# Feature-major x for the first projection of a two-layer hybrid trunk, loaded in blocks beside the first weights on a second DMA queue

## The chip, the core and the metric

The kernel runs on one core of a Trainium2 chip. The metric is the device time of one execution in microseconds (us); each version is run several times and the median is compared. Engines are named as in the profile: PE (TensorE matmul), PEld (TensorE weight load), DVE (VectorE), ACT (ScalarE), POOL (GpSimd), SP (SyncE, which here only issues DMAs). A `q` behind an engine's name (SPq, ACTq) means its instruction queue issuing DMAs.

## The reference

A residual stream `h` of 256 tokens by 1024 features (float32) goes through two layers: a dilated-attention mixer, a SwiGLU FFN, a forgetting-attention mixer, a second FFN, and a final RMSNorm. The change touches the first projection alone:

```python
def rmsnorm(x, g):
    y = xf * lax.rsqrt(jnp.mean(xf * xf, axis=-1, keepdims=True) + RMS_EPS) * g
    return y

def dilated_mixer(h, w_in, w_out):
    proj = (h @ w_in).reshape(B, S, N_GROUPS, 3, N_HEADS, HEAD_DIM)   # 1024 x 9216 weights
    ...

for i in range(DEPTH):
    ...
        h = h + dilated_mixer(rmsnorm(h, a_norm[j]), a_w_in[j], a_w_out[j])
    ...
return rmsnorm(h, final_norm)
```

## The kernel before, in words

**Precision.** Every float32 product is made of three matmuls in the fast fp32r type (`mm3`): each operand is split into a rounded high part and a remainder, and high x high, high x low and low x high are summed. So each block of weights, once landed in a `raw` tile, is "cut": ACT copies it to `wh` (L71) and DVE subtracts to get `wl` (L72).

**Weights.** `piece` loads one 1 MB block of weights into two `raw` tiles of 512 KB and cuts them. `raw` has 5 buffers, `wh` and `wl` 4 each. `weights` hands out a block and issues the load of the ones up to two ahead. The first projection consists of 36 units of 256 output columns (`a_units`): the first two, called unit 0 and unit 1 here, are the values of the second and third dilation group; from unit 2 on come queries and keys. For one unit, `proj_tok` runs 2 token tiles x 8 depth blocks x 3 matmuls = 48 matmuls of 256 columns.

**The beginning.** The norm's gain `g_a` is multiplied into x while it is transposed; the per-token factor 1/rms (`r_a`) is applied later, where the projections leave PSUM (L229) and in the rotary tables (`rb`, L459: a matmul that broadcasts `r_a` over partitions with the identity `ident`). The x rows (permuted, `x_perm`, tiles `xp0` and `xp1`, two DMAs of 256 KB each) are transposed on PE in 16 blocks of 128x128 (L310). ACT scales them out of PSUM into the high part of `xt` (L313) and DVE makes the low part (L315). Unit 0's weights are loaded in four parts of 256 KB and cut through the list `cuts`, two after each half tile. After the first token tile's transposes, the first halves of units 0 and 1 (`lead`) run; then come the second tile's transposes and the second halves. The sums of squares for `r_a` (`sq`, ACT, L147, then POOL, L138 and L141) are placed with `tc.issue_after(last.ins)`, where `last` is the last ACT scaling of x: on the engine of that instruction, ACT, nothing of the block may stand ahead of it. A few matmuls on a zeroed tile (`warm_up`, L278) run before data is there.

**What sets the order.** The program is written in one order, and a scheduler then orders the instructions of each engine by priority and by its own estimate of when inputs are ready; `first()` and `tc.high_priority` raise priorities. The resulting order is fixed: each engine runs its list strictly in that order, and an instruction that waits holds up all behind it on that engine. A DMA is issued from the list of its engine (SP before the change for all loads), so a load too can stand behind a waiting instruction.

Of the kernel before, what the change touches and what calls it, by code (L numbers as in the profile page):

```python
# [31 lines left out]
def trunk(ctx: ExitStack, tc: tile.TileContext, T, out):  # L32
# [39 lines left out]
            nc.vector.tensor_tensor(view(lo), src, view(hi).bitcast(F32), op=ALU.subtract)  # L72


    def piece(key, parts=2, todo=None):
        if key[0][:2] == "dn" and key[1] == LATE:
            wh, wl = (y.rearrange("p k c -> p (k c)") for y in fm_tile("ot", KT, 1))
        else:
            wh, wl = (wp.tile([P, 2048], F32R, tag=y, name=y, bufs=4) for y in ("wh", "wl"))
        n = 1024  # L80
        for c in range(2):
            raw = wp.tile([P, n], F32, tag="raw", name="raw", bufs=5)
            m = 2 * n // parts
            for i in range(parts // 2):
                v, u = slice(i * m, (i + 1) * m), slice(c * n + i * m, c * n + (i + 1) * m)
                nc.sync.dma_start(raw[:, v], T[key[0]][key[1]][:, u])
                cut = lambda raw=raw, v=v, u=u: split((wh, wl), lambda y: y[:, u], raw[:, v], False)
                if todo is None:
                    cut()
                else:  # L90
                    todo.append(cut)
        return wh, wl
# [124 lines left out]
    def values_a(v, g, o):  # L217

        if g == 0:
            v[0] = v_tile(o, [rt[:, t:t + 1] for t in range(2)])  # L220
            return
        for a in range(2):
            if 1 + a not in v:
                v[1 + a] = ap.tile([P, 512], F32, tag="v", name="v", bufs=6)
            rows = slice(a * 64, a * 64 + 64)
            with first():
                for t in range(2):
                    s = slice(t * S, (t + 1) * S)
                    nc.scalar.activation(v[1 + a][(g - 1) * 64:g * 64, s], o[rows, s], AF.Copy, scale=r_a[t][rows])  # L229

    def exps(s, nm, den, j):
        nc.scalar.activation(s, s, AF.Exp, bias=nm[:, j:j + 1], accum_out=den[:, j:j + 1])  # L232
# [43 lines left out]
    def warm_up(n):  # L276
        for i in range(n):
            nc.tensor.matmul(o[:, :S], warm[:, :P], warm[:, P:P + S], start=True, stop=True)  # L278

    warm_up(3)  # L280
    with tc.high_priority(offset=1000):
        nc.scalar.activation(warm[:, P + S:P + S + 1], mhalf, AF.Square)

    ident = const("ident", [P, P])
    xperm = [hrow(f"xp{t}") for t in range(2)]

    def load_x(t):
        for i in range(2):
            nc.sync.dma_start(xperm[t][:, i * 512:(i + 1) * 512],
                              T["x_perm"][t * P:(t + 1) * P, i * 512:(i + 1) * 512])  # L290

    load_x(0)
    g_a = const("g_a", [P, KT])
    cuts = []
    ready[order[0]] = piece(order[0], 4, cuts)
    state["next"] = 1
    load_x(1)
    xt = xt_tile()

    r_a = []  # L300

    def scaled_t(t):
        for half in range(2):
            tr = psum("tr")
            hi, lo = xt
            ks = range(half * 4, half * 4 + 4)
            c = slice(t * P, (t + 1) * P)
            src = {k: tr[:, k % 4 * P:(k % 4 + 1) * P] for k in ks}
            for k in ks:
                tp = nc.tensor.transpose(src[k], xperm[t][:, k * P:(k + 1) * P], ident)  # L310
            with first():
                for k in ks:
                    last = nc.scalar.activation(hi[:, k, c], src[k], AF.Copy, scale=g_a[:, k:k + 1])  # L313
                for k in ks:
                    nc.vector.scalar_tensor_tensor(lo[:, k, c], src[k], g_a[:, k:k + 1], hi[:, k, c].bitcast(F32),  # L315
                                                   op0=ALU.mult, op1=ALU.subtract)
                for _ in range(min(2, len(cuts))):
                    cuts.pop(0)()
        if t == 0:
            with tc.issue_after(tp.ins):  # L320
                warm_up(4)
        return last

    for t in range(2):
        last = scaled_t(t)
        if t == 0:
            lead = []
            for i in range(2):
                wt = weights("a_in", a_units[i][1] * 3 + 2)
                lead.append((wt, psum("mm")))  # L330
                proj_tok(xt, wt, lead[i][1][:, :S], 0)
    with tc.issue_after(last.ins):
        for t in range(2):
            r_a.append(rstd([sq(xperm[t])]))
# [104 lines left out]
    for i, (hq, g, w) in enumerate(a_units):  # L439
        if i % 9 == 0:  # L440
            quad = {"hq": hq, "fm": {}, "pt": {}, "v": {}, "nm": stat_tile("nm", 24), "den": stat_tile("den", 24)}
        wt, o = lead[i] if i < 2 else (weights("a_in", hq * 9 + g * 3 + w), psum("mm"))
        if i == 1:
            rcos = const("rcos", [P, S])
            rsin = const("rsin", [P, S])
# [7 lines left out]
        if w < 2:  # L453
            for c in range(2):
                proj_feat(xt, wt, o[:, c * S:(c + 1) * S], c)
            if i == 2:
                rb = psum("tr")
                for t in range(2):
                    nc.tensor.matmul(rb[:, t * P:(t + 1) * P], r_a[t].to_broadcast([P, P]), ident,  # L459
                                     start=True, stop=True)  # L460
                for c in (rcos, rsin):
                    nc.vector.tensor_tensor(c, c, rb[:, :S], op=ALU.mult)
                rt = ap.tile([P, 2], F32, tag="rt", name="rt", bufs=1)
                tmp = ap.tile([P, D], F32, tag="xn", name="rd", bufs=2)[:, :S].rearrange("p (b c) -> p b c", b=2)
                e = early(rb[:, :S], None)
                nc.vector.tensor_tensor(tmp, e, ident[:, None, :].to_broadcast([P, 2, P]), op=ALU.mult)
                nc.vector.tensor_reduce(rt, tmp, axis=AX.X, op=ALU.add)
            q = rotated(o, f"fm{w}", nc.vector if g == 0 else nc.gpsimd)
            if g == 0:
                y = ap.tile([P, 2, 2, S], F32R, tag="h", name="qkr", bufs=4)  # L470
                f, q = q, (y[:, 0], y[:, 1])
                split(q, lambda y: y, f)
            quad["fm"][g, w] = q
            if w == 1:
                later(i + 1, scores_a, quad, g)
                if g == 2:
# [390 lines left out]
```

## Time and profile before

| what | value |
|---|---|
| device time, median of 3 runs | 806.12 us (805.39 to 806.36) |
| profiled execution, its own time | 805.15 us |
| span of its trace | 803.4 us |
| PE busy | 787.4 us (98%) |
| DVE busy | 555.4 us (69%) |
| ACT busy | 421.2 us (52%) |
| data moved by DMA | 135.00 MB, mean 168 GB/s |

The span runs from the first to the last recorded instruction; 1.75 us of the execution lie around it. PE busy is an upper reading, since matmuls are pipelined and overlap in the record. The first 22.3 us of the span hold the beginning described above: loads, transposes, and units 0 and 1.

### The profile page before, as it was taken

To read this page: it belongs to the slowest core of one execution; us is meant where nothing else is said; L and a number is where in the kernel's file an instruction comes from. 1 tells how busy PE (TensorE), PEld (TensorE's weight loads), DVE (VectorE), ACT (ScalarE), POOL (GpSimd) and SP (SyncE) were. 2 spreads that over 40 slices of the span, in tenths; PEclk is the share of its full clock that TensorE was granted. 3 is DMA by queue.
4 is the path that set the end of the run, shared out by engine and by line. 5 is a ranking of instruction groups with operands and counts; after the bars stand their busy time and mean duration, and the time that the engine had idled before them with its cause. 6 is when DMAs were issued, how large, how long until landed. Compare 5 with 4: busy or idle time off the path is not lost.

```text
span 803.4 us, 13954 instructions
## 1 busy us (share of the span) xinstructions
PE 787.4 (98%) x5564; PEld 702.4 (87%) x5564; DVE 555.4 (69%) x829; ACT 421.2 (52%) x819; POOL 59.9 (7%) x76
## 2 busy tenths in 40 slices
PE   8999999999999999999999999999999999999996
PEld 7989899899999789888888879988879888888885
DVE  6798997986986685555657555677766756556643
ACT  7756347447445365455556545364535655546532
POOL 0010111011010110000000001211111000000001
PEclk9999999999999999999999999999999999999999
DMA  8856253734634346655556434543316665655601
GB/s 293 271 158 217 79 184 109 251 106 141 211 130 159 105 162 211 208 180 189 179 205 230 165 133 146 184 171 130 95 40 236 212 207 171 198 179 205 218 1 52
DMA packets 38833, 135.00 MB, mean 168 GB/s; under 512 B 4592, under 2 KB 5360, under 8 KB 38768
## 3 DMA queue, kind: packets, MB, share of 16 engines
q1 hardware_dynamic: 38624, 133.85, 49.9%
q8 instruction: 43, 0.70, 0.3%
q10 hardware_dynamic: 144, 0.26, 0.1%
q14 instruction: 22, 0.18, 0.1%
HBM read 133.05 MB, written 1.05 MB: 167 GB/s over the span
## 4 chain that ended last, share of the span: by engine, by line
PE 82%; DVE 10%; ACT 3%; issue 3%; DMA 1%; SPq 0%; POOL 0%; POOLq 0%; DVEq 0%
PE ps_mm L167 10%; PE ps_mm L169 10%; PE ps_mm L168 10%; PE ps_tr L198 9%; PE ps_mm L198 9%; PE ps_tr L199 4%; PE ps_mm L199 4%; PE ps_sc L167 4%; PE ps_sc L168 4%; PE ps_sc L169 4%; DVE wl L72 4%; PE ps_o L167 3%; PE ps_o L168 3%; PE ps_o L169 3%; ACT wh L71 2%
## 5 line engine op out<-in xcount | busy, mean ns | idle before, releaser
L72 DVE TENSOR_TENSOR wl<-raw,wh 128x1024 fp32r<-128x1024 f32 (+1 forms) x242 | 299.7, 1256 | 133.9 <-ACT wh L71 133.7
L71 ACT ACTIVATE wh<-raw 128x1024 fp32r<-128x1024 f32 (+1 forms) x242 | 248.3, 1048 | 165.2 <-issue 51.6
L167 PE MATMUL ps_mm<-xt,wh 128*128 128x256 f32 x512 | 147.4, 288 | 0.0
L168 PE MATMUL ps_mm<-xt,wh 128*128 128x256 f32 x512 | 145.4, 284 | 0.0
L169 PE MATMUL ps_mm<-xt,wl 128*128 128x256 f32 x512 | 145.4, 284 | 0.0
L198 PE MATMUL ps_tr<-xt,wh 128*128 128x512 f32 x304 | 109.6, 400 | 0.0
L198 PE MATMUL ps_mm<-xt,wh 128*128 128x512 f32 x304 | 108.1, 396 | 0.0
L167 PEld LDWEIGHTS ps_mm<-xt,wh 128*128 128x128 f32 x512 | 97.9, 191 | 3.1 <-issue 2.3
L168 PEld LDWEIGHTS ps_mm<-xt,wh 128*128 128x128 f32 x512 | 98.0, 191 | 1.5 <-issue 1.5
L169 PEld LDWEIGHTS ps_mm<-xt,wl 128*128 128x128 f32 x512 | 97.9, 191 | 1.0 <-issue 1.0
L167 PE MATMUL ps_mm<-wh,xt 128*128 128x256 f32 x304 | 86.6, 285 | 0.8 <-ACT wh L71 0.8
L168 PE MATMUL ps_mm<-wl,xt 128*128 128x256 f32 x304 | 86.0, 284 | 0.3 <-DVE wl L72 0.3
L169 PE MATMUL ps_mm<-wh,xt 128*128 128x256 f32 x304 | 85.8, 283 | 0.0
L199 PE MATMUL ps_tr<-xt,wl 128*128 128x256 f32 x304 | 85.1, 280 | 0.0
L199 PE MATMUL ps_mm<-xt,wl 128*128 128x256 f32 x304 | 84.9, 279 | 0.0
L198 PEld LDWEIGHTS ps_tr<-xt,wh 128*128 128x128 f32 x304 | 57.1, 188 | 15.1 <-DVE low L557 1.5
L198 PEld LDWEIGHTS ps_mm<-xt,wh 128*128 128x128 f32 x304 | 57.1, 188 | 13.2
L232 ACT ACTIVATE p<-p,nm 128x64 f32<-128x64 f32 (+2 forms) x128 | 51.4, 407 | 29.3 <-DVE nm L241 17.9
L167 PEld LDWEIGHTS ps_mm<-wh,xt 128*128 128x128 f32 x304 | 58.5, 192 | 1.7 <-ACT wh L71 1.4
L168 PEld LDWEIGHTS ps_mm<-wl,xt 128*128 128x128 f32 x304 | 58.4, 192 | 0.7 <-DVE wl L72 0.5
L169 PEld LDWEIGHTS ps_mm<-wh,xt 128*128 128x128 f32 x304 | 58.4, 192 | 0.0
L199 PEld LDWEIGHTS ps_mm<-xt,wl 128*128 128x128 f32 x304 | 57.2, 188 | 0.5
(213 smaller groups left out, 1271.5 us busy)
## 6 DMA issues: line engine op xcount, KB each, us to landing
raw<-in_gu SPq DMA_DIRECT2D x88, 512.0 KB, 4.3
raw<-in_a_in SPq DMA_DIRECT2D x70, 512.0 KB, 4.6
raw<-in_dn SPq DMA_DIRECT2D x44, 512.0 KB, 4.0
raw<-in_b_in SPq DMA_DIRECT2D x24, 512.0 KB, 4.6
raw<-in_a_out SPq DMA_DIRECT2D x8, 512.0 KB, 3.6
raw<-in_b_out SPq DMA_DIRECT2D x8, 512.0 KB, 3.5
grow<-in_norms SPq DMA_DIRECT2D x4, 512.0 KB, 5.6
xp<-in_x_perm SPq DMA_DIRECT2D x4, 256.0 KB, 4.6
```

Of the source, the lines that this page charges most:

```text
L71: nc.scalar.activation(view(hi), src, AF.Copy)
L72: nc.vector.tensor_tensor(view(lo), src, view(hi).bitcast(F32), op=ALU.subtract)
L167: nc.tensor.matmul(o, sh, mh, start=start, stop=False)
L168: nc.tensor.matmul(o, sh, ml, start=False, stop=False)
L169: return nc.tensor.matmul(o, sl, mh, start=False, stop=stop)
L198: nc.tensor.matmul(o.rearrange("p (x s) -> p x s", x=2), wh, xt.full[:, k], start=k == 0, stop=False)
L199: nc.tensor.matmul(o[:, :S], wl, xt[0][:, k], start=False, stop=k == KT - 1)
L232: nc.scalar.activation(s, s, AF.Exp, bias=nm[:, j:j + 1], accum_out=den[:, j:j + 1])
```

## The change

The host hands over x a second time, laid out feature-major (`x_fm`: 128 partitions of features, 8 depth blocks of 256 tokens). It is loaded on SP in four parts of 256 KB (two depth blocks each) into tiles `xf0` and `xf1`, behind `g_a`. Unit 0's weights, in four parts of 256 KB, are issued from ACT instead of SP (`piece` gets a parameter `eng`). The 16 transposes are gone: for each depth block, ACT scales x from `xf` into the high part of `xt`, DVE makes the low part, and every second block one part of unit 0's weights is cut. Unit 0 is written depth block by depth block for both token tiles, into two PSUM tiles (`lead`, tag `sc`); unit 1 is now an ordinary unit. `ident` and the token-major x (`xp0`, `xp1`, now one 512 KB DMA each) are still loaded, behind `x_fm`, since the sums of squares and the broadcast use them. The squares are still inside `tc.issue_after(last.ins)`, but `last` is now the last matmul of unit 0, a PE instruction. There are four warm-up matmuls instead of three and four.

```diff
-    def piece(key, parts=2, todo=None):
+    def piece(key, parts=2, todo=None, eng=nc.sync):
...
-                nc.sync.dma_start(raw[:, v], T[key[0]][key[1]][:, u])
+                eng.dma_start(raw[:, v], T[key[0]][key[1]][:, u])
...
-                    nc.scalar.activation(v[1 + a][(g - 1) * 64:g * 64, s], o[rows, s], AF.Copy, scale=r_a[t][rows])
+                    src = o[t][rows, :S] if isinstance(o, list) else o[rows, s]
+                    nc.scalar.activation(v[1 + a][(g - 1) * 64:g * 64, s], src, AF.Copy, scale=r_a[t][rows])
...
-    warm_up(3)
+    warm_up(4)
     with tc.high_priority(offset=1000):
         nc.scalar.activation(warm[:, P + S:P + S + 1], mhalf, AF.Square)
 
+    xf = [hrow(f"xf{i}") for i in range(2)]
+    g_a = const("g_a", [P, KT])
+    for i in range(4):
+        c = slice(i % 2 * 512, i % 2 * 512 + 512)
+        nc.sync.dma_start(xf[i // 2][:, c], T["x_fm"][:, i * 512:(i + 1) * 512])
+    cuts = []
+    w0 = piece(order[0], 4, cuts, nc.scalar)
+    ready[order[1]] = piece(order[1])
+    state["next"] = 2
+    xt = xt_tile()
+
+    r_a = []
+    lead = [psum("sc") for _ in range(2)]
+    hi, lo = xt
+    for k in range(KT):
+        src = xf[k // 4][:, k % 4 * S:(k % 4 + 1) * S]
+        with first():
+            nc.scalar.activation(hi[:, k], src, AF.Copy, scale=g_a[:, k:k + 1])
+            nc.vector.scalar_tensor_tensor(lo[:, k], src, g_a[:, k:k + 1], hi[:, k].bitcast(F32),
+                                           op0=ALU.mult, op1=ALU.subtract)
+            if k % 2 == 0:
+                cuts.pop(0)()
+        for t in range(2):
+            last = mm3(lead[t][:, :S], both(xt, ALL, k, slice(t * P, (t + 1) * P)),
+                       both(w0, ALL, slice(k * 256, (k + 1) * 256)), k == 0, k == KT - 1)
     ident = const("ident", [P, P])
     xperm = [hrow(f"xp{t}") for t in range(2)]
-
-    def load_x(t):
-        for i in range(2):
-            nc.sync.dma_start(xperm[t][:, i * 512:(i + 1) * 512],
-                              T["x_perm"][t * P:(t + 1) * P, i * 512:(i + 1) * 512])
-
-    load_x(0)
-    g_a = const("g_a", [P, KT])
-    cuts = []
-    ready[order[0]] = piece(order[0], 4, cuts)
-    state["next"] = 1
-    load_x(1)
-    xt = xt_tile()
-
-    r_a = []
-
-    def scaled_t(t):
...
-        if t == 0:
-            with tc.issue_after(tp.ins):
-                warm_up(4)
-        return last
-
     for t in range(2):
-        last = scaled_t(t)
-        if t == 0:
-            lead = []
-            for i in range(2):
-                wt = weights("a_in", a_units[i][1] * 3 + 2)
-                lead.append((wt, psum("mm")))
-                proj_tok(xt, wt, lead[i][1][:, :S], 0)
+        nc.sync.dma_start(xperm[t], T["x_perm"][t * P:(t + 1) * P, :])
     with tc.issue_after(last.ins):
         for t in range(2):
             r_a.append(rstd([sq(xperm[t])]))
...
-        wt, o = lead[i] if i < 2 else (weights("a_in", hq * 9 + g * 3 + w), psum("mm"))
+        if i == 0:
+            o = lead
+        else:
+            wt, o = weights("a_in", hq * 9 + g * 3 + w), psum("mm")
...
-            for t in range(i < 2, 2):
+            for t in range(2 if i else 0):
                 proj_tok(xt, wt, o[:, t * S:(t + 1) * S], t, g == 0)
...
+    t["x_fm"] = x[perm].T.reshape(KT, P, S).transpose(1, 0, 2).reshape(P, KT * S)
```

How the scheduler orders the engines' lists changes with it, at three places. From unit 2 on, the lists of the two kernels are almost the same. A number behind a name is the tile's own: `raw_88`, `raw_91` (before) and `raw_89`, `raw_92` (now) hold unit 0's weights, cut to `wh_86` and `wh_87`; `raw_137`, `raw_141` and `raw_97`, `raw_101` unit 1's, cut to `wh_135` and `wh_95`.

ACT before, from its first x scaling on:

```order
L313 ACTIVATE xt_96<-ps_tr_97,g_a_84 128x128 x4
L313 ACTIVATE xt_96<-ps_tr_114,g_a_84 128x128 x4
L71 ACTIVATE wh_86<-raw_88 128x512 x2
L71 ACTIVATE wh_86<-raw_91 128x512 x2
L313 ACTIVATE xt_96<-ps_tr_215,g_a_84 128x128 x4
L71 ACTIVATE wh_135<-raw_137 128x1024
L313 ACTIVATE xt_96<-ps_tr_228,g_a_84 128x128 x4
L71 ACTIVATE wh_135<-raw_141 128x1024
L71 ACTIVATE wh_145<-raw_147 128x1024
L147 ACTIVATE junk_241,ssq_242<-xp0_80 128x1024
```

ACT now, from its start on:

```order
L86 DMA raw_89<-in_a_in 128x512
L283 ACT_TABLE_LOAD
L283 ACTIVATE warm_71<-mhalf_67 128x1
L86 DMA raw_89<-in_a_in 128x512
L303 ACTIVATE xt_105<-xf0_79,g_a_81 128x256 x4
L303 ACTIVATE xt_105<-xf1_80,g_a_81 128x256 x4
L86 DMA raw_92<-in_a_in 128x512 x2
L147 ACTIVATE junk_186,ssq_187<-xp0_182 128x1024
L147 ACTIVATE junk_192,ssq_193<-xp1_183 128x1024
L71 ACTIVATE wh_95<-raw_97 128x1024
L71 ACTIVATE wh_87<-raw_89 128x512 x2
L71 ACTIVATE wh_87<-raw_92 128x512 x2
```

Unit 0's cuts stood directly behind the first tile's scaling; now all of x's scaling, the issue of unit 0's last two parts, both squares of the token-major x and the cut of unit 1's first half stand ahead of them. The squares stood behind three cuts of 1024 columns.

SP now, the loads in the order of their issue:

```order
L60 DMA g_a_81<-in_g_a 128x8
L290 DMA xf0_79<-in_x_fm 128x512 x2
L290 DMA xf1_80<-in_x_fm 128x512 x2
L60 DMA ident_180<-in_ident 128x128
L314 DMA xp0_182<-in_x_perm 128x1024
L314 DMA xp1_183<-in_x_perm 128x1024
L86 DMA raw_97<-in_a_in 128x1024
L86 DMA raw_101<-in_a_in 128x1024
```

The 1 MB of token-major x, which stood in two halves around unit 0's weights, now stands between the feature-major x and unit 1's weights.

PE now, its first rows (`ps_sc_106` and `ps_sc_107` are unit 0's two token tiles, `ps_mm_228` is unit 1, `rs_189` and `rs_195` are `r_a`):

```order
L279 MATMUL ps_o_73<-warm_71 128x256 x4
L445 MATMUL ps_tr_348<-ident_180,rs_189 128x128
L445 MATMUL ps_tr_348<-ident_180,rs_195 128x128
L167 MATMUL ps_mm_228<-wh_95,xt_105 128x256
L167 MATMUL ps_sc_106<-wh_87,xt_105 128x256
L167 MATMUL ps_sc_107<-wh_87,xt_105 128x256
L168 MATMUL ps_mm_228<-wl_96,xt_105 128x256
L169 MATMUL ps_mm_228<-wh_95,xt_105 128x256
L167 MATMUL ps_mm_228<-wh_95,xt_105 128x256
L168 MATMUL ps_mm_228<-wl_96,xt_105 128x256
L169 MATMUL ps_mm_228<-wh_95,xt_105 128x256
L168 MATMUL ps_sc_106<-wl_88,xt_105 128x256
```

Before, PE had 3 warm-ups, 8 transposes and 4 warm-ups ahead of unit 0's first matmul, and the broadcast of `r_a` stood inside unit 2. Now the broadcast of both `r_a` stands ahead of every projection matmul, and eight matmuls of units 0 and 1 stand ahead of the one that needs unit 0's first low part (`wl_88`); 88 of the 96 matmuls of the two units come from there on. On DVE the low part of unit 1's first half (`wl_96`) stands directly ahead of unit 0's four low parts (`wl_88`).

More of the change, by code (lines that the diff above doesn't have):

```diff
@@ L284, in trunk @@
     ident = const("ident", [P, P])
     xperm = [hrow(f"xp{t}") for t in range(2)]
-    def load_x(t):
-        for i in range(2):
-            nc.sync.dma_start(xperm[t][:, i * 512:(i + 1) * 512],
-                              T["x_perm"][t * P:(t + 1) * P, i * 512:(i + 1) * 512])
-    load_x(0)
-    g_a = const("g_a", [P, KT])
-    cuts = []
-    ready[order[0]] = piece(order[0], 4, cuts)
-    state["next"] = 1
-    load_x(1)
-    xt = xt_tile()
-    r_a = []
-    def scaled_t(t):
[L303 to L318, printed above, removed]
-        if t == 0:
-            with tc.issue_after(tp.ins):
-                warm_up(4)
-        return last
```

## The prediction, written before the changed kernel was run

> **What bounds the kernel now.** I read the page first (busy time and the chain of waits), then the table of windows, then the timeline of the first 23 us engine by engine.
>
> ```profile
> PE 787.4 (98%) x5564; PEld 702.4 (87%) x5564; DVE 555.4 (69%) x829; ACT 421.2 (52%) x819; POOL 59.9 (7%) x76
> PE 82%; DVE 10%; ACT 3%; issue 3%; DMA 1%; SPq 0%; POOL 0%; POOLq 0%; DVEq 0%
> ```
>
> ```profile
> 0.00:22.30 22.30, 19.05 (x126) 17.02 (x126) 12.52 (x27) 15.82 (x35) 2.26 (x10) 1.00 0.84 289
> 22.30:40.00 17.70, 17.70 (x149) 17.70 (x149) 15.26 (x23) 12.73 (x16) 0.00 (x0) 1.00 0.80 273
> 40.00:60.00 20.00, 19.85 (x170) 17.49 (x169) 18.60 (x27) 10.83 (x24) 3.81 (x3) 1.00 0.52 159
> 80.00:100.00 20.00, 18.95 (x161) 17.00 (x159) 19.39 (x32) 7.25 (x14) 3.33 (x3) 1.00 0.24 80
> ```
>
> The second number in a window's row is its length, the third PE's busy time. PE carries 82% of the chain, and from 22.3 us it has nothing idle until 40 and 0.15 us until 60. So whatever moves the start of unit 2 moves the end by about as much. The beginning is worth looking at, and there it is the start of unit 2 that I have to time.
>
> ```profile
> 1.30 2.93 PE L278 MATMUL ps_o<-warm 128*128 128x256 f32 x6 [1.30 <-DVE warm L273]
> 5.34 1.89 PE L278 MATMUL ps_o<-warm 128*128 128x256 f32 x8
> 8.03 0.38 PE L167 MATMUL ps_mm<-wh,xt 128*128 128x256 f32 x1 [0.79 <-ACT wh L71]
> 8.75 0.39 PE L168 MATMUL ps_mm<-wl,xt 128*128 128x256 f32 x1 [0.34 <-DVE wl L72]
> 10.55 0.44 PE L310 MATMUL ps_tr<-ident,xp 128*128 128x128 f32 x2 [0.82 <-DMA xp<-in_x_perm]
> 22.14 0.28 PE L168 MATMUL ps_mm<-wl,xt 128*128 128x256 f32 x1
> 22.26 0.28 PE L169 MATMUL ps_mm<-wh,xt 128*128 128x256 f32 x1
> 22.38 0.32 PE L167 MATMUL ps_mm<-xt,wh 128*128 128x256 f32 x1
> ```
>
> A timeline row is start, duration, engine, line. Unit 0 begins at 8.03 and unit 2 at 22.38. Matmuls of 256 columns start 0.12 us apart (22.14, 22.26, 22.38), so the 96 matmuls of units 0 and 1 need 11.5 us of the 14.35; the second tile's transposes and waits take the rest. At most 2.8 us could be had between these two marks, and a little by an earlier start.
>
> **The change part by part.** The diff reads as if the blocks of x and of weights arrived in pairs and PE began with the first pair. The order of the engines' lists says otherwise: unit 0's first cut on ACT stands behind both squares of the token-major x and behind the cut of unit 1's first half, and PE's first matmul behind the broadcast of `r_a`. Strictly ordered lists make PE's start wait for the seventh load on SP, `raw_97`. So I time that load.
>
> Loads. What did the beginning move, and when did it land?
>
> ```profile
> 4.46 0.91 SPq L289 DMA_DIRECT2D xp<-in_x_perm  x2
> xp<-in_x_perm SPq DMA_DIRECT2D x1, 256.0 KB, 6.2
> raw<-in_a_in SPq DMA_DIRECT2D x1, 512.0 KB, 7.7
> 4.00:5.00 1.00, 1.00 (x6) 0.80 (x6) 0.00 (x0) 0.00 (x0) 0.00 (x0) 1.00 0.86 245
> 5.00:6.00 1.00, 1.00 (x8) 0.92 (x8) 0.00 (x0) 0.79 (x4) 0.00 (x0) 1.00 0.49 74
> 6.00:7.00 1.00, 1.00 (x6) 0.76 (x4) 0.61 (x3) 1.00 (x6) 0.00 (x0) 1.00 0.74 168
> 10.00:11.00 1.00, 0.45 (x4) 0.46 (x5) 0.96 (x2) 0.51 (x1) 0.00 (x0) 1.00 1.10 406
> 13.00:14.00 1.00, 1.00 (x10) 0.94 (x9) 0.87 (x4) 1.00 (x3) 0.00 (x0) 1.00 1.04 426
> ```
>
> The last number of a load's row is the time from issue to landing in us, that of a window GB/s. The last part of x (second of the two from 4.46, so issued near 4.9) landed 6.2 us later, at 11.1, when 64 + 4 + 1024 + 1024 = 2116 KB had been asked for up to it. Now SP asks for the same 2116 KB up to the end of `xp1`, but unit 0's weights come on top from ACT: 512 KB early, 512 KB after x's scaling. Those 512 to 1024 KB (0.52 to 1.05 MB) take 1.3 to 2.6 us at 0.41 MB/us: `xp1` lands at 12.4 to 13.7, I take 13.0. `raw_97`, 0.52 MB more, lands 1.25 us later, at 14.2. From below: the dip to 74 and 168 GB/s between 5 and 7 us costs about 1.4 us against its neighbours (2 us at 121 instead of some 400 is 0.56 MB, at 400); if it doesn't come back, 12.8, and with the last 512 KB behind it 12.2. From above: `raw_97` can't be issued before `xf1`'s first part has freed its DMA semaphore, near 7.5, and the slowest 512 KB load here took 7.7: 15.2. That ACT takes four issues off SP is worth nothing, because SP's list is not what is late.
>
> The Trainium skill says the same of the second queue (DMA: Bandwidth & Descriptors, "Issuing engines are not separate DMA queues"): loads from different engines share the same 16 DMA engines, and only sequencer time is saved; by the opposite view the token-major x would not delay unit 0's weights at all, yet the sum here would stay, since it hangs on `raw_97`, which is on SP's own queue.
>
> ACT, DVE, POOL. Their prices stand in these rows:
>
> ```profile
> 7.34 0.63 ACT L71 ACTIVATE wh<-raw 128x512 fp32r<-128x512 f32 x1
> 12.97 1.08 ACT L71 ACTIVATE wh<-raw 128x1024 fp32r<-128x1024 f32 x1
> 16.81 1.11 ACT L147 ACTIVATE junk<-xp 128x1024 f32<-128x1024 f32 x1
> 17.85 1.10 ACT L71 ACTIVATE wh<-raw 128x1024 fp32r<-128x1024 f32 x1
> 8.01 0.69 DVE L72 TENSOR_TENSOR wl<-raw,wh 128x512 fp32r<-128x512 f32 x1
> 14.17 1.22 DVE L72 TENSOR_TENSOR wl<-raw,wh 128x1024 fp32r<-128x1024 f32 x1
> 20.08 0.19 POOL L138 TENSOR_SCALAR rs<-ssq 128x1 f32<-128x1 f32 x1 [0.70 <-ACT junk L147]
> 20.35 0.55 POOL L141 TENSOR_TENSOR rs<-rs,mhalf 128x1 f32<-128x1 f32 x1
> ```
>
> The second square, from 13.0, takes 1.04 us to the next ACT instruction (16.81 to 17.85): 14.1. The cut of unit 1's first half begins with its landing, 14.2, and ends at 15.3 (1.08); `r_a` comes meanwhile (0.19 + 0.55 plus gaps, 15.0). Then unit 0's first high part: 15.9. DVE: `wl_96` 15.3 to 16.5 (1.22), then unit 0's first `wl_88` until 17.2 (0.69, before the overlap of neighbours; I take 17.1). That is the moment that decides. ACT delivers the further parts of unit 0 every 0.55 to 0.63 us and DVE every 0.6 to 0.69, while PE uses one for 12 matmuls, 1.44 us, so nothing more is late; the last weights of unit 1 land near 15.5 and are cut by 20.2, and PE wants them after 23.
>
> PE. 88 matmuls from 17.1 at 0.12 us are 10.6 us: unit 2 at 27.7 instead of 22.38, +5.3 us. The removed transposes (the second tile's eight, some 1 us of the old stretch) are in that difference already, and so are the warm-ups, which end before data is there.
>
> The clock. The six warm-up rows at the start took 2.93 us (0.49 each), the eight later ones 1.89 us (0.24 each): an array that comes from idling runs at half pace for its first 3 to 4 us. Now the warm-ups end near 5 and PE idles for 10 us. No row shows what that does, as PE never idles that long later; the nearest is the start. Like there, matmuls would cost 0.24 instead of 0.12 from 15.3 to near 19, of which 2 to 2.5 us lie behind 17.1: a loss of about half, 1.2 us. Bounds: 0 (the profile's granted clock stands at 1.00 in every window) and 2.0 (4 us, all after 17.1). I take 1.2, since the warm-up rows are the same array after the same kind of pause. Sum: +6.5 us.
>
> The Trainium skill has a rule for that (TensorE: Matmul & The Clock Gate, Part 1: The HAM clock gate): after an idle window of about 3.4 us the clock falls to half and needs as long of activity to return. By it the loss would be some 1.7 us, an estimate, and the sum +7.0; the start's rows agree with it, and no row here shows the fall after a pause.
>
> What could come back later? Loads go on while PE waits, so units 2 to 4 would be cut earlier, relative to PE, than before. But PE was not waiting for cuts from 22.3 to 60 anyway; the 1.05 us missing between 80 and 100 could shrink at most. I count nothing.
>
> Result: 805.15 + 6.5 = 811.65 us for the profiled execution's kind; that one lies 0.97 below the median of 806.12, so 812.6 for the median.
>
> **The rivals.** *The pairs arrive as the diff reads, and it is faster.* If the first part of x and of weights sufficed, PE could begin near 6 (both land near 4, then 0.63 and 0.69 for the cut), unit 0 would end near 12, and unit 1, free to follow, near 18: -4.5 us, 801.6. The mechanism must bring `raw_97` and `xp1` early, since ACT's list puts them ahead: to break even, the 88 matmuls must start at 22.38 - 10.6 = 11.8, so `raw_97` must land at 8.9. By then 3.2 MB would have to be in, of which the best rate here, 426 GB/s, brings 3.0 MB from 2 us on. Chance 3%, with 2% for a tie.
>
> *Two queues fill better and the clock holds.* The dip at 5 to 7 us stood behind the small `g_a` load and may be due to it or to first touches; now `g_a` goes first. With `raw_97` at 12.2 everything up to PE moves 2 us, and without the slow clock the sum is +3.3 us, 809.4; either one alone gives 810.6 to 811.4. For it: windows of over 400 GB/s later. Against: every load has as many bytes ahead as before or more. Chance 28%.
>
> *Later still.* `raw_97` at 15.2 and 2.0 us of slow clock: +8.3, 814.4; a new wait in the first units on top (the PSUM tiles `sc` of unit 0 are emptied on ACT behind the weights' cuts) could bring 816. Chance 12%.
>
> **How the numbers follow.** Main case 55% (811.5 to 813.7), early 28%, late 12%, faster 3%, tie 2%. A difference of 0.2%, 1.6 us here, is what a measurement of this kernel can tell from none; every slower case lies beyond it. So slower 0.95, same 0.02, faster 0.03. The range reaches from just below the early case to the late one with its extra wait: 809.0 to 816.0. It leaves out the two small cases on the other side and the tails of early and late.
>
> **What would show it.** In the changed profile ACT's first cut must be that of unit 1 (1024 columns), behind the two squares, near 14; PE idle from about 5 to about 15; the first unit 0 matmul with `wl` near 17; unit 2 near 28 to 29. The clock shows in the starts of the first matmuls: 0.24 apart if I am right, 0.12 if not. The loads' step is wrong if `raw_97` lands before 12 or after 15.5, and the whole is wrong if unit 0's matmuls start before 11.8. The span from unit 2 on should be as long as before (803.4 - 22.4 = 781.0 us); if it is shorter by more than 1 us, the delay was partly won back and my "nothing" was wrong.

## The result, and the profile after

| | before | changed |
|---|---|---|
| device time, median of 6 runs each | 805.75 us (804.86 to 806.36) | 809.57 us (808.62 to 810.58) |
| profiled execution | 805.15 us | 810.58 us |
| span of its trace | 803.4 us | 808.8 us |

The ratio is 1.0044, with a 95% interval of 1.0031 to 1.0058. The changed kernel is slower by 3.8 us; the prediction had +6.5 us and a range from 809.0 to 816.0. First the page of the changed kernel, the busy time:

```profile
PE 786.5 (97%) x5542; PEld 701.9 (87%) x5542; DVE 554.5 (69%) x821; ACT 420.3 (52%) x811; POOL 59.0 (7%) x76
```

PE has 0.9 us less to do (787.4 before) in a span that is 5.4 us longer: the work did go away, and PE's idle time grew by 6.3 us, from 16.0 (803.4 - 787.4) to 22.3. The table of windows shows where (start and end, length, then the busy time of PE, PEld, DVE, ACT and POOL, the granted clock, the DMA share and GB/s):

```profile
10.00:19.00 9.00, 5.32 (x20) 4.53 (x21) 4.67 (x8) 7.04 (x12) 1.49 (x4) 0.50 0.86 322
28.80:40.00 11.20, 11.20 (x96) 11.20 (x95) 9.77 (x12) 7.00 (x10) 0.00 (x0) 1.00 0.88 312
40.00:60.00 20.00, 20.00 (x149) 18.33 (x149) 17.50 (x27) 11.13 (x24) 2.60 (x2) 1.00 0.55 181
```

From 28.8 to 60 us PE has nothing idle, as before from 22.3. All that is lost is lost ahead of unit 2, and from 10 to 19 the granted clock stands at 0.50, where every window of the kernel before that the prediction shows has 1.00. The timeline of PE in that stretch (start, duration, engine, line; in brackets the idle time and what ended it):

```profile
13.22 0.79 PE L445 MATMUL ps_tr<-ident,rs 128*128 128x128 f32 x2 [8.13 <-POOL rs L141]
...
17.49 0.41 PE L168 MATMUL ps_sc<-wl,xt 128*128 128x256 f32 x1
17.70 0.41 PE L169 MATMUL ps_sc<-wh,xt 128*128 128x256 f32 x1
...
19.55 0.28 PE L167 MATMUL ps_sc<-wh,xt 128*128 128x256 f32 x1
19.67 0.28 PE L168 MATMUL ps_sc<-wl,xt 128*128 128x256 f32 x1
```

PE idles 8.13 us behind its warm-ups, since the broadcast of `r_a` stands first in its list. The first unit 0 matmul with a low part starts at 17.49 (foretold: 17.1). Matmuls start 0.21 us apart until 19.41, then 0.12. Unit 2's first matmul is at 28.89. What ACT did meanwhile:

```profile
11.10 1.06 ACT L147 ACTIVATE junk<-xp 128x1024 f32<-128x1024 f32 x1 [0.95 <-DMA xp<-in_x_perm]
...
13.89 2.62 ACT L71 ACTIVATE wh<-raw 128x1024 fp32r<-128x1024 f32 x4 [0.38 <-DMA raw<-in_a_in]
```

Its first cut, at 13.89, is that of unit 1's first half (1024 columns lead the group), behind both squares, and it waited for that load: `raw_97` landed at 13.9. Unit 0's first weights had been there since 4.2, as the first row of the chain of waits shows (start, length, what):

```profile
0.72 3.50 DMA raw<-in_a_in
4.23 8.10 DMA xp<-in_x_perm
12.36 1.16 ACT junk L147 x2
...
14.48 0.80 PE ps_tr L445 x2
```

By the chain, the second half of the token-major x (landed at 12.3), its square and the broadcast of `r_a` release PE; the cut of `raw_97` (13.89 + 1.08 = 14.97) is level with them. Two paths end at 15.0, which matters for the first experiment that takes one of them away.

### The profile page after: what moved, and what is told of

Same layout as the page of the kernel before. It is cut to its first block, busy times and chain, and to the rows that moved or that the text cites. A ratio compares the mean times of both kernels' runs of the same rounds, so it can differ in the third digit from the quotient of the medians.

```text
span 808.8 us, 13900 instructions
## 1 busy us (share of the span) xinstructions
PE 786.5 (97%) x5542; PEld 701.9 (87%) x5542; DVE 554.5 (69%) x821; ACT 420.3 (52%) x811; POOL 59.0 (7%) x76
## 3 DMA queue, kind: packets, MB, share of 16 engines
HBM read 134.10 MB, written 1.05 MB: 167 GB/s over the span
## 4 chain that ended last, share of the span: by engine, by line
PE 84%; DVE 9%; ACT 3%; issue 3%; DMA 1%; POOL 0%; POOLq 0%; DVEq 0%
PE ps_mm L167 10%; PE ps_mm L169 10%; PE ps_mm L168 10%; PE ps_tr L198 9%; PE ps_mm L198 9%; PE ps_sc L167 5%; PE ps_tr L199 4%; PE ps_mm L199 4%; PE ps_sc L168 4%; PE ps_sc L169 4%; DVE wl L72 3%; PE ps_o L168 3%; PE ps_o L167 3%; PE ps_o L169 3%; PE ps_o L266 1%
## 5 line engine op out<-in xcount | busy, mean ns | idle before, releaser
L167 PE MATMUL ps_mm<-wh,xt 128*128 128x256 f32 x288 | 82.3, 286 | 0.0
L168 PE MATMUL ps_mm<-wl,xt 128*128 128x256 f32 x288 | 81.9, 284 | 0.0
L169 PE MATMUL ps_mm<-wh,xt 128*128 128x256 f32 x288 | 81.7, 284 | 0.0
L198 PEld LDWEIGHTS ps_mm<-xt,wh 128*128 128x128 f32 x304 | 57.1, 188 | 13.5
L233 ACT ACTIVATE p<-p,nm 128x64 f32<-128x64 f32 (+2 forms) x128 | 51.4, 406 | 33.1 <-DVE nm L242 21.7
L199 PEld LDWEIGHTS ps_tr<-xt,wl 128*128 128x128 f32 x304 | 57.4, 189 | 0.0
L168 PEld LDWEIGHTS ps_mm<-wl,xt 128*128 128x128 f32 x288 | 55.7, 193 | 0.4 <-DVE wl L72 0.2
L167 PEld LDWEIGHTS ps_mm<-wh,xt 128*128 128x128 f32 x288 | 55.7, 193 | 0.4
```

Of the source, the lines that this page charges most:

```text
L167: nc.tensor.matmul(o, sh, mh, start=start, stop=False)
L168: nc.tensor.matmul(o, sh, ml, start=False, stop=False)
L169: return nc.tensor.matmul(o, sl, mh, start=False, stop=stop)
L198: nc.tensor.matmul(o.rearrange("p (x s) -> p x s", x=2), wh, xt.full[:, k], start=k == 0, stop=False)
L199: nc.tensor.matmul(o[:, :S], wl, xt[0][:, k], start=False, stop=k == KT - 1)
```

## The experiments

All times are medians; the ratio is to the kernel before on the same chip. "Unit 2" is the start of its first matmul in the profiled execution, "weights" the start of DVE's first `e<-nm,mn` (the weights that combine the dilation groups, at 73 to 81 us, a mark that every kernel has), and "end" the span. The last three columns come from one profiled execution each.

| run | time, us | ratio (95%) | unit 2 | unit 2 to weights | weights to end |
|---|---|---|---|---|---|
| before | 805.75 | 1 | 22.38 | 53.0 | 728.0 |
| before_b | 805.95 | 1.0001 | 22.87 | 53.0 | 728.1 |
| before_c | 806.56 | 1.0002 | 22.96 | 53.0 | 729.2 |
| changed | 809.57 | 1.0044 (1.0031 to 1.0058) | 28.89 | 51.9 | 728.0 |
| again | 809.41 | 1.0040 (1.0027 to 1.0053) | 27.89 | 51.9 | 727.6 |
| warm21 | 808.95 | 1.0033 (1.0022 to 1.0044) | 26.84 | 52.3 | 728.1 |
| sqlate | 811.04 | 1.0058 (1.0045 to 1.0070) | 28.30 | 52.8 | 728.1 |
| w0sp | 809.92 | 1.0043 (1.0030 to 1.0056) | 27.61 | 52.3 | 727.7 |
| w1late | 809.26 | 1.0043 (1.0024 to 1.0062) | 27.21 | 52.5 | 728.2 |
| w0first | 803.34 | 0.9961 (0.9948 to 0.9975) | 20.23 | 52.8 | 727.9 |
| w0warm8 | 803.02 | 0.9961 (0.9949 to 0.9974) | 19.99 | 53.4 | 727.8 |
| w0warm11 | 802.94 | 0.9960 (0.9947 to 0.9974) | 20.52 | 53.0 | 727.8 |

The last column is the first finding: behind the weights every kernel takes 727.6 to 728.2 us, but for one execution of the kernel before. Whatever these kernels differ in arises in the first 81 us.

**again: the changed kernel, unaltered.**

> The changed kernel itself once more, for a second profile and more times. The prediction's sum said +6.5 us; the profiled pair shows +5.4 (810.58 against 805.15), the medians +3.8. If the beginning alone sets the difference and the profiled execution was an unlucky one, this profile should again have unit 2 start near 28 to 29 us (22.4 before), with a scatter of about 1 us that follows from when the seventh SP load (unit 1's first half) lands and how long the granted clock stays at 0.50. If something late in the program gives time back in most runs, unit 2 starts at 28.9 again and the span behind it is over 1 us shorter than 779.9. Expected: +3 to +5.5 us against the kernel before, PE's first projection matmul at 14 to 15.5.

809.41 us, 3.0 us above the kernel before on that chip, and PE's first projection matmul at 14.59, both as expected. Unit 2 came 1.0 us earlier than in the first profile, just ahead of the expected 28 to 29. Timeline of PE:

```profile
17.07 0.41 PE L168 MATMUL ps_sc<-wl,xt 128*128 128x256 f32 x1
...
17.50 0.36 PE L168 MATMUL ps_sc<-wl,xt 128*128 128x256 f32 x1
17.70 0.29 PE L169 MATMUL ps_sc<-wh,xt 128*128 128x256 f32 x1
```

0.42 us of that is the earlier first low part (17.07 for 17.49), the rest the slow pace, which ends at 17.6 here and at 19.5 there. One profiled execution is thus good for unit 2 to about 1 us, no better.

**warm21: is the slow pace the pause's doing?** Enough warm-ups that PE hardly pauses.

```diff
-    warm_up(4)
+    warm_up(21)
```

> The changed kernel with 21 warm-up matmuls instead of 4, nothing else: PE is kept busy on a zeroed tile from 1.3 us to about 13. The clock theory: the 20 matmuls that started 0.21 apart between 15.0 and 19.4 now start 0.12 apart, and unit 2 comes 1.2 us earlier, near 27.7; the time falls by about 1.2 us against the changed kernel. Rival, the clock costs nothing because PE waits for cuts anyway: the starts are 0.12 apart but PE stands idle between the four parts of unit 0, and unit 2 stays at 28.5 or later; time within 0.4 us of the changed kernel. If 21 are too many, the broadcast of r_a starts later than 13.9 and part of the gain is lost.

PE's timeline:

```profile
1.30 11.88 PE L279 MATMUL ps_o<-warm 128*128 128x256 f32 x42 [1.30 <-DVE warm L274]
...
15.81 0.28 PE L169 MATMUL ps_mm<-wh,xt 128*128 128x256 f32 x1
15.93 0.28 PE L167 MATMUL ps_mm<-wh,xt 128*128 128x256 f32 x1
...
16.28 0.29 PE L168 MATMUL ps_sc<-wl,xt 128*128 128x256 f32 x1
```

The matmuls start 0.12 us apart, the 88 from 16.28 take exactly the 10.56 us that 0.12 each makes, and PE doesn't stand idle between the four parts of unit 0, as the rival had it. Unit 2 comes 1.05 us earlier than in again, and earlier than the 27.7 expected; part of that is earlier loads, so the pace is better read from the first projection matmul to unit 2: 12.52 us here (14.32 to 26.84), 13.30 in again (14.59 to 27.89), 13.89 in the first profile (15.00 to 28.89). So the pause does cost the pace: 0.8 us in again, 1.4 in the first profile. The prediction gave it 1.2, all of it behind the first low part. There it is 0.26 us in again and 0.84 in the first profile (10.82 and 11.40 against 10.56); in both another 0.5 lies ahead of it. The time fell by 0.5 us only, where 1.2 was expected, with intervals that overlap: 0.4 us is lost again between unit 2 and the weights, which is taken up under the reasons.

**sqlate: are the squares what ACT's cuts wait for?** The squares go behind unit 0's last cut (`split` returns its ACT instruction).

```diff
-                cuts.pop(0)()
+                cut = cuts.pop(0)()
...
-    with tc.issue_after(last.ins):
+    with tc.issue_after(cut.ins):
```

> The changed kernel with the two squares tied behind unit 0's last cut on ACT instead of behind a PE instruction (which held nothing on ACT); loads in the same order. Theory of the loads: ACT's first cut waits for unit 1's first half, which lands near 13.9, so taking the squares (13.5 at their end) away moves it by less than 0.5 us; the broadcast of r_a goes back into a later unit and costs 0.45 there; the time stays within 0.6 us of the changed kernel. Theory of the squares: the misplaced squares are what holds ACT, 2.5 us of work ahead of the first cut; then the first cut starts 2 us or more earlier and the time falls by about 2 us.

ACT's timeline:

```profile
12.84 2.82 ACT L71 ACTIVATE wh<-raw 128x1024 fp32r<-128x1024 f32 x4 [3.16 <-DMA raw<-in_a_in]
```

With no square ahead of it, the first cut still waited 3.16 us for its load, to 12.84. So the squares are not what holds it; that this is 0.6 us earlier than in again is the load, which lands at different times in kernels with the same order of loads (see w0sp). PE began at 13.95 and had the first low part at 16.01, 1.06 us earlier than in again, but it ran at half pace up to 19.4, and unit 2 came at 28.30. The time grew by 1.6 us against again, where a change of at most 0.6 was expected; of the 1.8 us between the two spans 0.4 is there at unit 2, 0.9 comes from there to the weights, and 0.5 in the last stretch, where kernels that are alike differ by as much. The column "unit 2 to weights" rose from 51.9 to 52.8: the broadcast of `r_a`, now late, went back into PE's busy time (at 34.06), which the expectation had, and the first scores take longer again, which it hadn't. Both are taken up under the reasons.

**w0sp: the second queue alone undone.** Unit 0's loads go back to SP; the scheduler then puts them and unit 1's ahead of the token-major x.

```diff
-    w0 = piece(order[0], 4, cuts, nc.scalar)
+    w0 = piece(order[0], 4, cuts)
```

> The second queue alone undone: unit 0's four loads go out on SP, everything else as changed. The scheduler then puts unit 0's and unit 1's weights ahead of the token-major x and the squares behind the first cuts. Theory of the loads: unit 1's first half has 1 MB less ahead of it and lands near 10.7 instead of 13.9, the first unit 0 matmul with a low part starts near 13.7 instead of 17.5, and unit 2 near 25.5; about 3.3 us less than the changed kernel, so within 1 us of the kernel before. Rival, that the feature-major path itself is what costs (1 MB more to move, no overlap of halves): the time stays within 1 us of the changed kernel. Rival, that the second queue helps to fill the DMA engines: slower than the changed kernel.

ACT's timeline:

```profile
12.80 4.08 ACT L71 ACTIVATE wh<-raw 128x1024 fp32r<-128x1024 f32 x6 [4.65 <-DMA raw<-in_a_in]
```

And the windows:

```profile
6.00:8.50 2.50, 0.00 (x0) 0.00 (x0) 2.50 (x7) 2.15 (x6) 0.00 (x0) 0.83 0.79 168
8.50:18.00 9.50, 4.09 (x16) 3.62 (x17) 4.28 (x7) 5.20 (x9) 0.00 (x0) 0.51 1.02 401
```

The time is as in the changed kernel, not within 1 us of the kernel before as the theory of the loads had it. It fits the rival that the feature-major path itself costs; only w0first, below, rules that out. Nor is the queue alone undone, since the scheduler moved the token-major x and the squares with it: the two together neither gain nor cost what can be measured.

With the 1 MB of token-major x no longer ahead of it, `raw_97` should have landed at 10.7 by the prediction's count of bytes; it landed at 12.8. The windows show where the time went: 168 GB/s from 6 to 8.5 us, 401 behind it. Not even the microsecond against 13.9 can be put down to the order of the loads, since with that order unchanged it landed at 13.9, 13.5, 13.2 and 12.8 (changed, again, warm21, sqlate). So the count of bytes ahead, at 0.41 MB/us, came near the landing in the changed kernel without being the law. And the lists still do what they did: ACT's first cut is that of `raw_97`, though unit 0's four parts had landed from 9.5 to 11.5.

**w1late: unit 1 out of the way too.** To sqlate is added that unit 1's load and cut are written behind unit 0's.

```diff
-    ready[order[1]] = piece(order[1])
-    state["next"] = 2
...
+    with tc.issue_after(cut.ins):
+        ready[order[1]] = piece(order[1])
+    state["next"] = 2
```

> Two lists put right: the squares tied behind unit 0's last cut, and unit 1's weights written behind unit 0, so that ACT cuts unit 0's parts between x's scalings; the loads keep their queues, so unit 0's last two parts are still issued by ACT behind x's scaling. Theory: what sets PE's start is that unit 0's first cut stands behind unit 1's first half. Then PE begins at 6 to 7 us on the first part, stands still from about 10 until the last two parts have landed (16 to 17 in the changed kernel) and are cut, and unit 2 comes near 25.5, some 2.5 to 3 us ahead of the changed kernel: 806 to 807. Rival, the loads as a whole are what is late: unit 1's first half lands at 13.5 whatever is cut first, and unit 2 stays at 27.5 or later, within 1 us of the changed kernel.

ACT's timeline:

```profile
8.57 0.45 ACTq L87 DMA_DIRECT2D raw<-in_a_in  x1
...
14.62 0.63 ACT L71 ACTIVATE wh<-raw 128x512 fp32r<-128x512 f32 x1 [4.46 <-DMA raw<-in_a_in]
16.55 1.58 ACT L71 ACTIVATE wh<-raw 128x512 fp32r<-128x512 f32 x2 [1.30 <-DMA raw<-in_a_in]
```

PE began at 6.89, as the diff of the change reads, but halfway through unit 0 it stood still for 3.3 us: the last two parts of unit 0 are issued from ACT's own list behind x's scaling, at 8.2 and 8.6, and landed at 14.6 and near 16.5. The theory had this pause, but not that it brings the half pace back, until 21.7. So the time did not fall to the 806 to 807 expected: 809.26 is within 1 us of the changed kernel, which was the rival's mark (that the loads as a whole are late), though unit 2 at 27.21 came a little ahead of its 27.5. Taking one late item away let the next one through, at the same price.

**w0first: unit 0's four loads ahead of all else on ACT.** Added to w1late; the scheduler now puts unit 1's loads ahead of the token-major x as well.

```diff
-    w0 = piece(order[0], 4, cuts, nc.scalar)
+    with tc.high_priority(offset=2000):
+        w0 = piece(order[0], 4, cuts, nc.scalar)
```

> As the one before, and unit 0's four loads are issued from ACT ahead of everything else, which lets the scheduler put unit 1's weights ahead of the token-major x on SP. This is the pairwise arrival that the diff reads like. Theory: PE begins at 6 to 7, unit 0 ends near 12 to 13, unit 1's halves land near 11.5 and 13, and unit 2 starts at 19 to 20, 2.5 to 3 us ahead of the kernel before; the broadcast of r_a stands in a later unit again (0.45). 803 to 804.5, so 2 to 3 us faster than before. Rival, the loads of 2 KB rows are too slow for it (224 to 320 GB/s against 400 to 425 for 4 KB rows): unit 0 ends near 15, unit 2 near 22, as before; time within 1 us of the kernel before.

PE's timeline:

```profile
6.65 0.50 PE L168 MATMUL ps_sc<-wh,xt 128*128 128x256 f32 x2 [1.77 <-ACT wh L71]
...
8.36 0.42 PE L170 MATMUL ps_sc<-wh,xt 128*128 128x256 f32 x1
8.57 0.41 PE L168 MATMUL ps_sc<-wh,xt 128*128 128x256 f32 x1
```

803.34 us, 0.4% less than the kernel before and 0.8% less than the changed one, in the range that the theory gave (its profiled execution, 802.70, is the quickest of ten). The pairs of x and weights now arrive as the diff of the change reads; PE begins unit 0 at 6.65 and unit 2 at 20.23 (19 to 20 expected; unit 0 ends only at 14.5, for 12 to 13). The rival with slow loads had unit 2 near 22. All that separates this kernel from the changed one is the place of squares, loads and cuts in the three lists; its arithmetic is the same. That shows the mechanism of the loss: the order, not the layout of x or the 1 MB more that is loaded. The three edits were not tried in every combination, so the share of each stays open.

**w0warm8 and w0warm11: the half pace that is left there.** In w0first matmuls start 0.21 apart from 8.1 to 11.3. Eight or eleven warm-ups, in place of four, bridge the pause.

```diff
-    warm_up(4)
+    warm_up(8)
```

> The kernel with unit 0's pieces first, with 8 warm-up matmuls in place of 4, so that TensorE's pause ahead of unit 0 is about 0 instead of the 1.8 us there. Theory one (the clock still costs there: 3.3 us of matmuls start 0.21 apart instead of 0.12, so some 1.3 us): matmuls 0.12 apart from about 7 on, unit 2 near 19.0 instead of 20.23, time 802.0 to 802.8 against 803.34. Theory two (TensorE waits there for ScalarE's cuts anyhow, which end some 1.3 us apart): the matmuls are faster but the waits between them longer by the same, unit 2 within 0.4 of 20.23, time within 0.4 of 803.34.

> The same with 11 warm-up matmuls, which end behind the first cut: unit 0 starts up to 1 us later than with 8, but the clock has no pause to fall in. Theory one: unit 2 between 19.0 and 20.0, time 802.0 to 803.0. Theory two: unit 2 at 20.2 to 21.2, time 803.3 to 804.5, since the start is put off and the cuts set the pace.

PE's timeline with eight:

```profile
1.30 6.57 PE L280 MATMUL ps_o<-warm 128*128 128x256 f32 x16 [1.30 <-DVE warm L275]
7.52 0.59 PE L168 MATMUL ps_sc<-wh,xt 128*128 128x256 f32 x2
...
20.79 0.39 PE L170 MATMUL ps_mm<-xt,wl 128*128 128x256 f32 x1 [0.40 <-DVE wl L72]
```

The pace holds, as theory one has it: units 0 and 1 take 12.47 us (7.52 to 19.99) instead of 13.58. But unit 2, at 19.99 and 20.52, comes when theory two has it, since the warm-ups put the start off by 0.87 us. The times, 803.02 and 802.94 against a kernel before of 805.99 on that chip, are the same ratio as w0first's; taken as microseconds, the second falls into theory one's range, and 0.4 us can't be told apart here. The 0.24 us left at unit 2 are lost at once in a wait for its low part (0.40 at 20.79), which w0first does not have. ACT and DVE with eight:

```profile
16.40 2.00 ACT L231 ACTIVATE v<-ps_sc,rs 64x256 f32<-64x256 f32 x4
18.42 2.95 ACT L71 ACTIVATE wh<-raw 128x1024 fp32r<-128x1024 f32 x3
19.51 3.50 DVE L72 TENSOR_TENSOR wl<-raw,wh 128x1024 fp32r<-128x1024 f32 x3 [4.18 <-ACT wh L71]
```

DVE waits for ACT, and ACT's cut of unit 2's first half, at 18.42, waits for nothing: its weights had landed at 16.6, but both squares (from 14.07) and the four instructions that take unit 0's values out of PSUM stand ahead of it. So what PE meets next is again the order of ACT's list, not the weights. No run moves that cut forward.

**before_b and before_c: the kernel before, twice more.** No edit; they measure how far a single profile of it can be trusted.

> The kernel before once more, for a second profile. Its executions reach from 804.9 to 807.3 us and the profiled one was 805.15. If that scatter has its seat at the beginning, this profile's time should differ from 805.15 by as much as its unit 2 starts away from 22.38, and the span behind the first group weights (at 75.4 us) should be 728.0 again. If it doesn't, the scatter sits later.

> The same once more: a third profile, with the same expectation.

Their spans are 804.0 and 805.2 us, their unit 2 at 22.87 and 22.96. For before_b that is as expected: 0.6 us longer, of which 0.5 lie ahead of unit 2. Before_c is 1.8 us longer, and 1.2 of it arise behind the weights, where none was expected. The profile on which the prediction was made, with 22.38 and 803.4, was the quickest of three.

## Why the prediction was right, and where its size was off

**The loads and the lists: right.** The step said that strictly ordered lists make PE wait for the seventh load on SP. ACT's first cut was unit 1's, behind two squares; PE's list began with the broadcast; `raw_97` landed at 13.9 (14.2 foretold), the second part of the token-major x at 12.3 (13.0). w0first shows it from the other side: with these items out of the way the same work starts at 6.65.
The estimate behind the landing was weaker than its result. With this order of loads `raw_97` landed between 12.8 and 13.9 in four profiles, all ahead of the 14.2, and w0sp, with 1 MB less ahead of it, at 12.8 too. What did come as foretold is when it could be issued:

```profile
6.85 2.78 SPq L86 DMA_DIRECT2D raw<-in_a_in  x3
```

SP issued it when the third part of `x_fm` had landed, at 6.83 (near 7.5 foretold), and it took 7.0 us (7.7); in w0sp it went out at 4.94 and took 7.8.

**The moment that decides and unit 2: right in number, partly by luck.** 17.1 foretold, 17.49 and 17.07 measured. The prediction let DVE's first low part of unit 0 set this moment. DVE had it ready at 16.8 and 16.4 in the two profiles; PE came later because the matmuls ahead ran at half pace. The 88 matmuls from there took 11.40 us (10.6 + 1.2 foretold) and 10.82. Unit 2 was foretold at 28.9 (27.7 + 1.2) and came at 28.89 and 27.89: the first hits it more closely than one execution can be trusted.

**The clock: it fell as foretold, and 1.2 us lies between the two profiles.** By warm21 the half pace cost 0.8 us in again and 1.4 in the first profile (bounds 0 and 2.0). About 0.5 us of it lies ahead of the first low part, where the prediction had put none. The starts were 0.21 us apart, not 0.24.

**"I count nothing" for time that comes back: the step that failed.** The mark that the prediction set for it was the stretch from unit 2 to the end: 781.0 us, and wrong if shorter by more than 1 us. It was 779.9 (808.8 - 28.9) and 779.5 in again: 1.1 and 1.5 us shorter. The prediction saw that loads and cuts go on while PE waits, and put what comes back at nothing because PE was not waiting for cuts from 22.3 to 60 us. The two causes lie between unit 2 and the weights (53.0 to 51.9 in the table). The first is the broadcast of `r_a`. In the timeline of the kernel before it stands inside unit 2's dense matmuls:

```profile
28.05 0.28 PE L169 MATMUL ps_mm<-xt,wl 128*128 128x256 f32 x1
28.17 0.60 PE L459 MATMUL ps_tr<-ident,rs 128*128 128x128 f32 x4
28.53 0.36 PE L167 MATMUL ps_mm<-xt,wh 128*128 128x256 f32 x1
28.73 0.28 PE L168 MATMUL ps_mm<-xt,wh 128*128 128x256 f32 x1
```

From 28.05 to the matmul at 28.53 are 0.48 us where 0.12 would do, and 0.2 more to the next: about 0.45 us, which now lie in PE's idle time at 13 to 15 us. The second is at the first scores. The kernel before:

```profile
40.39 0.48 PE L167 MATMUL ps_sc<-qkr 64*128 64x256 f32 x2
40.79 0.39 PE L167 MATMUL ps_mm<-xt,wh 128*128 128x256 f32 x1
...
41.46 0.48 PE L168 MATMUL ps_sc<-qkr 64*128 64x256 f32 x2
...
42.78 0.39 PE L167 MATMUL ps_mm<-xt,wh 128*128 128x256 f32 x1
```

The changed kernel:

```profile
46.26 0.48 PE L167 MATMUL ps_sc<-qkr 64*128 64x256 f32 x2
...
47.82 0.39 PE L167 MATMUL ps_mm<-xt,wh 128*128 128x256 f32 x1
```

DVE's low part of `qkr` (the second of the two), before and changed:

```profile
L72 DVE TENSOR_TENSOR qkr<-fm,qkr x2: 689/690/691, 35.4 to 40.7; 128x512 fp32r<-128x512 f32 x2
```

```profile
L72 DVE TENSOR_TENSOR qkr<-fm,qkr x2: 676/680/683, 39.6 to 45.3; 128x512 fp32r<-128x512 f32 x2
```

Before, it ends at 41.4 (40.7 + 0.69), and the pair at 41.46 starts right behind it; PE's list has three projection matmuls in between. The six pairs take 2.39 us, or 2.03 without the three (0.36). Now it ends at 46.0, ahead of the first pair, the list has no other matmul between the pairs, and they take 1.56. That is 0.47 us, and with the broadcast 0.9 of the 1.1; the last 0.2 was not traced further. Two runs show what the 0.47 consist of. In w0first seven projection matmuls stand in between, and the low part is ready at 39.6, ahead of the second pair:

```profile
38.68 0.47 PE L168 MATMUL ps_sc<-qkr 64*128 64x256 f32 x2
...
40.11 0.48 PE L169 MATMUL ps_sc<-qkr 64*128 64x256 f32 x2
...
41.44 0.39 PE L168 MATMUL ps_mm<-xt,wh 128*128 128x256 f32 x1
```

The pairs take 2.76 us, or 1.92 without the seven. With no wait that is still 0.36 more than 1.56: so most of the 0.47 is what it costs to leave the scores and come back, which PE's list decides, and about 0.1 is the wait. In warm21 the pairs stand together as in the changed kernel, and the low part comes late, at 44.5:

```profile
44.20 0.47 PE L167 MATMUL ps_sc<-qkr 64*128 64x256 f32 x1
44.60 0.47 PE L168 MATMUL ps_sc<-qkr 64*128 64x256 f32 x1
```

There the scores take 1.97 us (to 46.17), so the wait alone cost 0.4: that is what warm21 lost behind unit 2. The prediction had looked for such time in windows where PE was idle; here PE was "busy" (19.85 of 20 us), yet with matmuls that started further apart. sqlate is the check: with the broadcast back among the matmuls (34.06) and three matmuls back between the scores, 0.9 of the 1.1 us is gone again.

**The reference: the other part of the size.** The sum was put on the profiled execution of before and carried over as a difference. 5.4 us is the difference of the two first spans, 3.8 that of the medians. Of the 1.6 between them, 0.6 is that the profiled before (805.15) lay below its later median (805.75), and 1.0 that the profiled changed run (810.58), the slowest of its six, lay above its own (809.57). So 6.5 foretold = 3.8 measured + 1.1 that came back + 1.6 of single executions. The last had been seen as 0.97 us and added to both sides, where it cancels; the kernel before starts unit 2 at 22.4 to 23.0, and the mean of three, 22.7, would have given 0.35 less.

**The rivals.** The time is close to what "two queues fill better and the clock holds" gave (809.4), and yet neither of its two conditions held: `raw_97` landed at 13.9 and not 12.2, and the clock fell. That the time comes close is luck. "Pairs arrive as the diff reads" needed `raw_97` at 8.9 and did not happen in the change; w0first takes unit 1's first half and the token-major x out of the way, so that the pairs do suffice, and measures 803.3 (801.6 foretold), short of it by 1.7 us. The half pace in it is not what is missing, since w0warm8 took it away and gained nothing that can be measured. "Later still" did not happen. What slows the transfers between 6 and 8.5 us in w0sp stays open: the kernel before has the same dip from 5 to 7 us, and in both the loads in 256 KB parts are under way then, but such a load was not measured by itself. In w0first, where the same parts are issued first and from ACT, no microsecond from 3 to 8 has less than 268 GB/s, so the size of the parts can't be the whole reason.

## What to carry to other kernels

Loading operands earlier and in pairs gains nothing while an unrelated item (here squares, a broadcast, the next unit's cut) stands ahead of their first use in one of three strictly ordered lists: read the lists first, and look for the latest load that any item ahead depends on. When such items are moved, move all of them, loads in compute engines' lists included, since clearing one only exposed the next here (sqlate and w1late gained nothing, w0first 0.8%). And take the size of an early delay from several profiles, and look behind it for work that falls into the new idle time or comes to stand ahead of its use: both together were 2.7 of the 6.5 us here.

## What the runs showed of the hardware

**The clock fell after a short pause too.** In w0first PE paused 1.77 us, ran one pair and waited another 0.23; windows of the granted clock:

```profile
7.50:8.00 0.50, 0.50 (x5) 0.50 (x6) 0.22 (x1) 0.46 (x2) 0.00 (x0) 0.96 1.05 406
8.00:8.50 0.50, 0.50 (x4) 0.50 (x4) 0.41 (x1) 0.50 (x3) 0.00 (x0) 0.50 1.10 406
...
11.50:12.00 0.50, 0.50 (x7) 0.50 (x6) 0.50 (x1) 0.50 (x2) 0.00 (x0) 1.00 1.04 399
```

The clock went to 0.50 at 8.0, while PE was busy again, and came back near 11.4. The Trainium skill (TensorE: Matmul & The Clock Gate, Part 1: The HAM clock gate) has the clock fall after at least one idle window of about 3.4 us. Here a pause of about half of that was enough. In w0warm8, without the pause, the pace held.

**How long the return takes varies.** From PE's first matmul behind the pause (in changed and again the broadcast) to the full pace went 4.0 us (w0sp, 13.91 to 17.9), 4.7 (again), 5.5 (sqlate), 6.3 (changed) and 6.4 (w1late, 15.30 to 21.7). The same section says that the return depends on where in the window the first matmul falls, by about 0.5 us either way; the runs agree that it varies, but by 2.4 us, and by 1.6 between two profiles of the same kernel (changed and again). It means that an earlier start can be worth nothing: sqlate had its first low part 1.06 us before again and unit 2 0.41 us behind it.

**The record of the clock can miss it.** In again the granted clock reads 1.00 in the window from 14 to 17 us, where matmuls start 0.21 apart:

```profile
14.00:17.00 3.00, 2.86 (x10) 2.38 (x11) 2.44 (x4) 2.23 (x5) 0.09 (x1) 1.00 0.81 282
```

The distance between starts is the safer reading.
